# Convolution rows through DRAM, a list ordered behind a pair of state updates, and 2.2 instead of 1.83 gather slots to 16 tokens of a build

## The chip, the cores and the metric

The kernel runs on one core of a Trainium2 chip. Its time is the device time of one execution in microseconds (us), median of three runs; the profile is that of one more execution. The core has TensorE (PE in the profile; PEld are its weight loads), VectorE (DVE), ScalarE (ACT), GpSimd (POOL), SyncE (SP, which only issues DMA here) and 16 DMA engines.

## What is computed

One layer: RetNet retention and a Conformer convolution share an input projection and an output projection; a PEER layer follows, which picks 16 experts of 16,384 for each of 8 heads by product keys. The inputs are a prompt of 512 tokens and 8 sampled sequences of 4 new tokens, each with a retention state and 30 cached convolution rows. Cut to what matters here:

```python
def retention(q, k, v, r0, log_gamma):          # chunks of 128 tokens
    ...
    def step(r, kv_n):
        return chunk_decay * r + kv_n, r         # the state's update
    ...

def conformer_conv(ca, cg, buf, dw_kernel, dw_bias, ln_g, ln_b):
    u = ca * jax.nn.sigmoid(cg)
    xpad = jnp.concatenate([buf, u], axis=1)
    y = lax.conv_general_dilated(xpad, dw_kernel[:, None, :], window_strides=(1,), padding='VALID',
        dimension_numbers=('NWC', 'WIO', 'NWC'), feature_group_count=CONV_WIDTH) + dw_bias   # 31 taps, 512 channels
    return jax.nn.silu(layer_norm(y, ln_g, ln_b)), xpad[:, -(CONV_K - 1):]

def peer(x2d, w_query, sub_keys_1, sub_keys_2, peer_u, peer_v):
    ...
    v1, i1 = lax.top_k(s1, PEER_TOPK)
    v2, i2 = lax.top_k(s2, PEER_TOPK)
    cand = (v1[..., :, None] + v2[..., None, :])...
    sv, ci = lax.top_k(cand, PEER_TOPK)
    ...
    act = jax.nn.gelu(jnp.einsum('phkd,pd->phk', u, xb), approximate=False)
    return jnp.einsum('phk,phkd->pd', gate * act, vv)
```

## The kernel before

The prompt's first 128 tokens (the first chunk) go through everything up to their expert lists first; the 32 sampled tokens and the other 384 prompt tokens follow. Experts are applied in two ways. For 256 of the later tokens every expert is multiplied densely, in 128 blocks (scores `sp`, L1021; products `pB`, L1216), with gates from matrices that are *built* on TensorE from the lists: for each token `B` (two halves, L1138) and `A` (L1117 or on ScalarE, L1122) are made, and L1157 multiplies them. For all other tokens an expert is a *slot*: GpSimd issues an indirect DMA that fetches for each of 128 tokens one expert's row of 2 x 1024 numbers (L730), VectorE takes the dot product (L736), ScalarE the gelu and the gate (L748, L753), and VectorE accumulates (L758). The first chunk has 128 slots (indices `I`), the sampled tokens 32 (`Is`, on 128 partitions), the last 128 prompt tokens 128 (`Ib`).

The first chunk's lists are made by five calls of `retrieve`, on heads 0, 1, 2-3, 4-5 and 6-7. Each takes the best 16 keys of both sides, converts their indices (L658), forms candidate sums (L663), and picks the best 16 with one-hot comparisons (L682 to L689). The list is copied to `I` at L866.

The stage that the change is about runs from 160 to 240 us. Two generators are woven there by `woven`, which advances one and then the other:

- `later_conv`, for the 384 later prompt tokens: four channel blocks `m` of the gated product `u_p` (`glu`: two projections, L255; sigmoid on ScalarE, L285; product on VectorE, L290); then the convolution as matmuls (`conv_taps`, L336), and the value projections (`project_v`, L384) between them. Four taps at a time are contracted over 128 partitions, 4 x 32 channels, so a tile of *rows* is needed that holds the channels of one block four times, each copy shifted by one token: `tap_rows` makes it with 16 copies of 32 x 412 on ScalarE (L325) per block, and the tap weights with one product on VectorE (L327). Two places of the tile `blk` hold the rows of even and of odd blocks in turn.
- `retain_s`, the sampled tokens' retention: for each pair of sequences the query against the state (L506), the key-value product (L512) and the state's update on VectorE (L514). The updates are appended to the list `updates`, sixteen in all, two for each pair of heads. The states lie in the tiles `states`, `xr` (of the first chunk) and `keys`; a pair's states are loaded at L472 and written out at L518.

The program's order on each engine is made when it is built, by a scheduler that goes by data dependences, priorities and a model of times; each engine then works through its own order strictly. `behind(a, b)` orders `a` after `b`. Two tables order the slots. SLOTS_BEHIND holds pairs (k, i): every dot from the k-th of the first chunk's dots so far on stands behind the i-th update. TURNS = (24, 1.83) does it for the last 128 slots during the second build: slot k from 24 on stands behind the build's turn int((k - 24) // 1.83) + 1, where a turn is 16 tokens.

Transfers issued by SyncE go out in its order: weights of the input projection (L152), states and results among them.

## Time and profile before

| | before |
|---|---|
| time, median of 3 runs (lowest to highest) | 1458.32 us (1458.04 to 1463.03) |
| the profiled execution's own time | 1455.97 us |
| its span | 1454.2 us |
| mean granted TensorE clock | 0.987 |
| moved by DMA | 506.78 MB, 348 GB/s over the span |

The profile is read on three levels. The page gives the busy time of each engine as a share of the span, and the chain of work that ended last, followed back from the end. A busy share is an average over stages with different limits, so the stages are read apart: a window gives the busy time of every engine in a stretch, the granted clock and the DMA share. Within a stage the timeline shows each instruction (or a run of equal ones, xcount) with its start, its length, and, in brackets, the idle time of its engine ahead of it and what ended that. A group has busy time, mean ns of one, and the idle time ahead of its instructions. L numbers are lines of the kernel before; behind the change the same lines stand some 8 to 15 lines further down (L325 has gone, and the others become L327 → L336, L336 → L345, L384 → L393, L506 → L515, L512 → L521, L514 → L523, L518 → L527, L658 → L667, L736 → L745, L758 → L767, L1117 → L1132, L1138 → L1153, L1157 → L1172, L1216 → L1231).

### The profile page before, as it was taken

What the parts mean: (1) busy time and instruction counts of PE and PEld (TensorE: products, weight loads), DVE (VectorE), ACT (ScalarE), POOL (GpSimd) and SP (SyncE); (2) the same over time, 40 slices, a digit from 0 to 9 for tenths busy, and PEclk for the clock granted to TensorE, in tenths of its full rate; (3) what the DMA queues carried; (4) which work ended last, traced back from release to release, by engine and by line L of the source; (5) the groups of instructions that cost most, each with busy time, mean ns of one, the idle gap of its engine ahead of it and who ended that gap; (6) DMA issues with size and microseconds to landing.
All of it is one profiled execution on the core that took longest, in us unless ns stands there. A gap on an engine that the chain in (4) does not pass through costs nothing.

```text
span 1454.2 us, 19716 instructions
## 1 busy us (share of the span) xinstructions
PE 1404.1 (97%) x6758; PEld 963.9 (66%) x6758; DVE 1162.1 (80%) x2796; ACT 492.8 (34%) x1455; POOL 427.4 (29%) x407
## 2 busy tenths in 40 slices
PE   8999889999999999998999999999999989999997
PEld 8887455568767588887888884444445656566443
DVE  5849858987769999979999996987676887666656
ACT  1424773363122232244555541214444211111111
POOL 2172124233432333222133312333221333222220
PEclk9999989999999999999999999999999999999999
DMA  9859759987898799998799989999998999999995
GB/s 350 311 203 376 247 204 385 369 327 282 322 396 319 265 364 402 377 405 316 238 405 366 370 309 359 415 416 384 334 359 327 378 418 418 415 392 412 414 397 197
DMA packets 100401, 506.78 MB, mean 348 GB/s; under 512 B 10279, under 2 KB 21287, under 8 KB 57413
## 3 DMA queue, kind: packets, MB, share of 16 engines
q0 software_dynamic: 43392, 309.32, 54.4%
q1 hardware_dynamic: 52157, 190.10, 34.4%
q10 hardware_dynamic: 4752, 6.11, 1.2%
q8 instruction: 53, 0.87, 0.2%
q14 instruction: 47, 0.39, 0.1%
HBM read 500.12 MB, written 5.80 MB: 348 GB/s over the span
## 4 chain that ended last, share of the span: by engine, by line
PE 50%; DVE 24%; DMA 14%; issue 5%; ACT 4%; POOL 1%; DVEq 0%; ACTq 0%; SPq 0%; POOLq 0%
PE pB L1216 25%; PE sp L1021 12%; PE mm L255 6%; DVE acc L758 6%; DMA g<-in_uv_dram,Ib 4%; DVE g L736 4%; DMA g<-in_uv_dram,I 4%; DMA uv<-in_ut_dram 3%; DVE g L316 2%; ACT blk L325 2%; PE mm L1157 2%; PE mm L583 1%; PE mm L336 1%; DMA cst<-in_consts_dram 1%; DMA ln<-in_uv_dram,I 1%
## 5 line engine op out<-in xcount | busy, mean ns | idle before, releaser
L1021 PE MATMUL sp<-x1T,uv 128*128 128x256 f32 x2048 | 465.8, 384 | 13.2 <-ACT W L1170 6.1
L1021 PEld LDWEIGHTS sp<-x1T,uv 128*128 128x128 f32 x2048 | 386.0, 191 | 81.8 <-issue 15.1
L758 DVE SCALAR_TENSOR_TENSOR acc<-g,wgt,acc 128x1024 f32<-128x1024 f32 x252 | 322.4, 1279 | 66.5 <-ACT wgt L753 64.5
L736 DVE SCALAR_TENSOR_TENSOR g<-g,x 128x1024 f32<-128x1024 f32 x255 | 309.0, 1217 | 77.3 <-DMA g<-in_uv_dram,Ib 49.4
L730 POOL DMA_INDIRECT g<-in_uv_dram,Ib x126 | 150.6, 1195 | 394.2 <-DVE acc L758 116.8
L748 ACT ACTIVATE act<-act 128x1 f32<-128x1 f32 x288 | 57.0, 201 | 577.6 <-DVE g L736 539.9
L730 POOL DMA_INDIRECT g<-in_uv_dram,I x104 | 135.9, 1307 | 296.9 <-DVE acc L758 176.9
L1216 PE MATMUL pB<-uv,Ga 128*128 128x512 f32 x352 | 158.7, 597 | 0.0
L255 PE MATMUL mm<-x1T,w 128*128 128x384 f32 (+1 forms) x448 | 152.9, 498 | 0.0
L255 PEld LDWEIGHTS mm<-x1T,w 128*128 128x128 f32 x448 | 84.5, 190 | 63.0 <-issue 31.6
L1216 PEld LDWEIGHTS pB<-uv,Ga 128*128 128x128 f32 x352 | 65.5, 190 | 70.8 <-issue 66.5
L1216 PE MATMUL pB<-uv,Gb 128*128 128x512 f32 x256 | 110.5, 593 | 0.0
L1216 PE MATMUL pB<-uv,Gd 128*128 128x512 f32 x256 | 110.0, 592 | 0.0
L1216 PEld LDWEIGHTS pB<-uv,Gb 128*128 128x128 f32 x256 | 48.3, 190 | 61.5 <-issue 57.1
L1216 PEld LDWEIGHTS pB<-uv,Gd 128*128 128x128 f32 x256 | 48.6, 190 | 60.9 <-issue 59.6
L1122 ACT ACTIVATE A<-row,e1T 128x128 f16<-128x128 bf16 x216 | 66.0, 391 | 45.5 <-PE mm L1157 45.1
L1216 PE MATMUL pB<-uv,Gc 128*128 128x512 f32 x160 | 71.5, 599 | 0.1
L255 PE MATMUL mm<-g,w 128*128 128x160 f32 (+1 forms) x512 | 65.3, 287 | 0.0
L255 PEld LDWEIGHTS mm<-g,w 128*128 128x128 f32 x512 | 64.4, 191 | 0.6
L730 POOL DMA_INDIRECT g<-in_uv_dram,Is x25 | 31.6, 1266 | 75.3 <-DVE acc L758 43.4
L1216 PEld LDWEIGHTS pB<-uv,Gc 128*128 128x128 f32 x160 | 29.3, 190 | 34.8 <-issue 33.0
L1170 ACT ACTIVATE W<-sp 128x256 f32<-128x256 f32 (+25 forms) x84 | 26.4, 314 | 73.2 <-PE sp L1021 70.9
(328 smaller groups left out, 1732.7 us busy)
## 6 DMA issues: line engine op xcount, KB each, us to landing
uv<-in_ut_dram SPq DMA_DIRECT2D x128, 512.0 KB
uv<-in_uv_dram SPq DMA_DIRECT2D x128, 512.0 KB
w<-in_w_in_dram SPq DMA_DIRECT2D x18, 1024.0 KB
w<-in_w_query_dram SPq DMA_DIRECT2D x15, 1024.0 KB
w<-in_w_out_dram SPq DMA_DIRECT2D x7, 1024.0 KB
ln<-in_ln_g_dram POOLq DMA_DIRECT2D x5, 512.0 KB
ln<-in_ln_b_dram POOLq DMA_DIRECT2D x5, 512.0 KB
g<-in_uv_dram,Ib POOLq DMA_INDIRECT x126
```

What stands on the lines that cost most here:

```text
L255: T.matmul(p[:, :n], w[m // 2][:, k, (m % 2) * 128:(m % 2 + 1) * 128], xT[:, k, c0:c0 + n], start=(k == 0), stop=(k == 7))
L316: V.scalar_tensor_tensor(y[:, m], u_p[:, m, p0 + k:p0 + k + L], dw[:, m, k:k + 1], y[:, m], op0=OP.mult, op1=OP.add)
L325: S.activation(rows[j * 32:j * 32 + 32, g], u_p[g * 32:g * 32 + 32, m, p0 + j:p0 + j + w], AF.Copy)
L730: fetch = G.indirect_dma_start(out=t, out_offset=None, in_=a["uv"], in_offset=bass.IndirectOffsetOnAxis(ap=idx[:, k:k + 1], axis=0))
L736: dot = V.scalar_tensor_tensor(t[:, :D], t[:, :D], 1.0, x1, op0=OP.mult, op1=OP.mult, accum_out=act[:, 0:1])
L748: gate_ = S.activation(act[:, 1:2], act[:, 0:1], AF.Gelu)
L758: V.scalar_tensor_tensor(acc, v, wgt, acc, op0=OP.mult, op1=OP.add)
L1021: mm = T.matmul(sp[:, i], u[:, k], x1T[:, k, NG2:], start=(k == 0), stop=(k == 7), skip_group_check=True)
L1122: made = S.activation(A[:, t], row, AF.Abs, bias=e1T[:, t1 + t:t1 + t + 1])
L1157: mm = T.matmul(pt[:, t % nt], A[t % TB], B[:, q, t % TB // 2, :, t % 2], start=(q == 0), stop=(q == 1))
L1170: S.activation(W[:, :n], sp[:, :n], AF.Gelu)
L1216: return [T.matmul(pB[b][q], W[:, b * 128:(b + 1) * 128], vt[:, q * 512:(q + 1) * 512], start=False, stop=(e == NK - 1), skip_group_check= ...
```

## The change

Four things. The row tiles of the convolution are no longer copied by ScalarE: each finished channel block of `u_p` is stored to DRAM (`store_u`, one DMA of 128 x 415 on ScalarE's queue, L322), and read back by four DMAs on SyncE's queue (L330), one for each shift, 32 partitions x 4 x 412. The loads are placed earlier than the copies were: those of a block go ahead of the block before it in the second loop. The tap weights are a function of their own. The conversion L658 of each list is kept in `placed`, and that of the first chunk's last list is ordered behind the first pair of state updates. And the two tables change their numbers. By TURNS, TensorE's order in the second build has for the most part 8 value products (two matmuls each in the profile) between the matmuls of 16 tokens, or 4 between those of 8, where it had 10; in VectorE's order dots and accumulations now stand between the two halves of some tokens' `B` too.

```diff
@@ -40,8 +40,8 @@
 FREE = 8
 TB_AT = {30: (0, 1), 36: (1, 1), 42: (2, 2), 50: (4, 2), 88: (6, 2)}
 SECOND = 34
-SLOTS_BEHIND = ((7, 1), (8, 3), (11, 5), (12, 7), (14, 9))
-TURNS = (24, 1.83)
+SLOTS_BEHIND = ((7, 1), (8, 3), (10, 5), (11, 7), (13, 9))
+TURNS = (24, 2.2)
 TURN = (90, 92)
 S_AT = 8
 GATED = 116
@@ -123,7 +123,7 @@
     banks = [ps0]
     turn = [0]
 
-    steps, updates = {}, []
+    steps, u_dram, updates, placed = {}, {}, [], []
 
     def mmps():
         turn[0] += 1
@@ -316,17 +316,26 @@
                 V.scalar_tensor_tensor(y[:, m], u_p[:, m, p0 + k:p0 + k + L], dw[:, m, k:k + 1], y[:, m],
                                        op0=OP.mult, op1=OP.add)
 
-    def tap_rows(m, L, p0, place):
+    def store_u(m, L, p0):
+
+        u_dram[m] = dr.tile([128, L + CK], F32, name=f"u_dram{m}")
+        nc.scalar.dma_start(u_dram[m], u_p[:, m, p0:p0 + L + CK])
+
+    def tap_rows(m, L, place):
 
         w = L + CK - 3
         rows = place[:, 0:4 * w].rearrange("p (g t) -> p g t", g=4)
-        for g in range(4):
-            for j in range(4):
-                S.activation(rows[j * 32:j * 32 + 32, g], u_p[g * 32:g * 32 + 32, m, p0 + j:p0 + j + w], AF.Copy)
+        by_group = u_dram[m].rearrange("(g c) t -> c g t", g=4)
+        for j in range(4):
+            nc.sync.dma_start(rows[j * 32:j * 32 + 32], by_group[:, :, j:j + w])
+        return rows
+
+    def tap_weights(m):
+
         taps = small("taps", [128, 32, 32], bufs=1)
         V.tensor_tensor(taps, cc("eye32").unsqueeze(1).to_broadcast([128, 32, 32]),
                         dwt[:, m].rearrange("p g k -> p (g k)").unsqueeze(2).to_broadcast([128, 32, 32]), op=OP.mult)
-        return rows, taps.rearrange("p (g k) c -> p g k c", g=4)
+        return taps.rearrange("p (g k) c -> p g k c", g=4)
 
     def conv_taps(y, m, L, rows, taps):
 
@@ -655,7 +664,7 @@
                 first = top16(vv[:n, j, s], iu[:n, j, s], sb[:n, s], NK)
                 if later:
                     later(first)
-        V.tensor_tensor(fi[:n], iu[:n], unit_k[:n].unsqueeze(1).unsqueeze(3).to_broadcast([n, nh, 2, TK]), op=OP.mult)
+        placed.append(V.tensor_tensor(fi[:n], iu[:n], unit_k[:n].unsqueeze(1).unsqueeze(3).to_broadcast([n, nh, 2, TK]), op=OP.mult))
         cand = pick("cand", [128, 2, nh, NCAND], bufs=1)
         both, src = cand.rearrange("p q h c -> p (q h) c"), vf.rearrange("p q h s k -> p (q h) s k")
         off = 0
@@ -891,17 +900,22 @@
         rows = {}
         for m in range(4):
             glu(W0[5], wca, xT, L, p0, ms=[m])
+            store_u(m, L, p0)
             yield
+            if m in (1, 3):
+                rows[m // 2] = tap_rows(m // 2, L, room[m // 2])
             if m == 1:
-                rows[0] = tap_rows(0, L, p0, room[0])
+                taps = tap_weights(0)
             if m == 2:
-                yield from conv_taps(y, 0, L, *rows[0])
+                yield from conv_taps(y, 0, L, rows[0], taps)
         w = load_win(2)
         for m in range(1, 4):
-            rows[m] = tap_rows(m, L, p0, room[m % 2])
+            if m < 3:
+                rows[m + 1] = tap_rows(m + 1, L, room[(m + 1) % 2])
+            taps = tap_weights(m)
             vs.append(project_v(w, xT, 128 * (m - 1)))
             yield
-            yield from conv_taps(y, m, L, *rows[m])
+            yield from conv_taps(y, m, L, rows[m], taps)
 
     banks[:] = [ps]
     r = slice(NS, n)
@@ -910,6 +924,7 @@
     for k, i in SLOTS_BEHIND:
         for dot in dots[k:]:
             behind(dot, updates[i])
+    behind(placed[4], updates[1])
     banks[:] = [ps]
     rope(load_win(0), 0, xT, n - NS, 160, [(0, n - NS, qT)])
     later_keys = rope_steps(load_win(1), 1, xT, n - NS, 160, [(0, n - NS, kT)])
```

Where the instructions stand now. In VectorE's order around the last list (names: `states` are the first pair's states, L514 and L523 their updates; `vf` is written by the conversion that starts a list's second half, L658 and L667; `u_p` is a gated product). Before, from the conversion to the first updates, with the rows between left to the sentence behind:

```order
L758 SCALAR_TENSOR_TENSOR acc<-g,wgt,acc 128x1024
L658 TENSOR_TENSOR vf<-iu,unit_k 128x64
L687 TENSOR_TENSOR oh<-oh 128x32x24
L696 TENSOR_TENSOR GT_135<-ex,sm 128x32
L663 TENSOR_TENSOR cand<-vf 128x4x16
```

```order
L686 TENSOR_TENSOR oh<-oh,ci 128x1600
L696 TENSOR_TENSOR GT_135<-ex,sm 128x32
L514 SCALAR_TENSOR_TENSOR states<-states,mm 128x2x128 x2
L687 TENSOR_TENSOR oh<-oh 128x32x24
L736 SCALAR_TENSOR_TENSOR g,act<-g,x_0_132 128x1024
L688 TENSOR_TENSOR oh<-oh 128x32x12
L689 TENSOR_REDUCE E_134<-oh 128x32
```

Behind the change:

```order
L698 TENSOR_REDUCE E_134<-oh 128x32
L875 CAST I_136<-E_134 128x32
L290 SCALAR_TENSOR_TENSOR u_p<-mm,cols,sg 128x384
L523 SCALAR_TENSOR_TENSOR states<-states,mm 128x2x128 x2
L667 TENSOR_TENSOR vf<-iu,unit_k 128x64
L745 SCALAR_TENSOR_TENSOR g,act<-g,x_0_132 128x1024
L672 TENSOR_TENSOR cand<-vf 128x4x16
```

The first pair's updates stood 27 rows behind the conversion, near the end of the last list; now they stand right ahead of the conversion, and the list before is finished ahead of them.

In TensorE's order of the same stage (L506 and L515 read the states, L512 and L521 multiply keys and values, L336 and L345 are the convolution's matmuls, L384 and L393 the value projection, L255 a projection). Before:

```order
L255 MATMUL mm<-x1T,w 128x384 x8
L506 MATMUL mm<-states,on 32x128 x8
L336 MATMUL mm<-blk,taps 32x384 x8
L512 MATMUL mm<-on,ktok 128x256 x2
L336 MATMUL mm<-blk,taps 32x384 x16
L506 MATMUL mm<-xr_862,on 32x128
L512 MATMUL mm<-on,ktok 128x256 x2
L506 MATMUL mm<-xr_862,on 32x128 x7
L336 MATMUL mm<-blk,taps 32x384 x8
L255 MATMUL mm<-x1T,blk 128x384 x7
```

Behind the change:

```order
L255 MATMUL mm<-x1T,w 128x384 x8
L515 MATMUL mm<-states,on 32x128 x8
L521 MATMUL mm<-on,ktok 128x256 x2
L515 MATMUL mm<-xr_862,on 32x128 x8
L521 MATMUL mm<-on,ktok 128x256 x4
L345 MATMUL mm<-blk,taps 32x384 x32
L255 MATMUL mm<-x1T,blk 128x384 x8
L255 MATMUL mm<-x1T,w 128x384 x8
L521 MATMUL mm<-on,ktok 128x256 x2
L393 MATMUL mm<-w,x1T 128x256 x16
```

The convolution's matmuls of block 0 lay between the key-value products; now they follow three pairs of these in one piece.

SyncE's order in the stage (L152 loads weights, L472 and L481 load states, L518 and L527 write them out). Before:

```order
L152 DMA w<-in_w_in_dram 128x2048 x5
L472 DMA keys<-in_state_retention_dram 128x8x128 x2
L518 DMA out_dram<-states 128x8x128
L152 DMA w<-in_w_in_dram 128x2048
L518 DMA out_dram<-xr_862 128x8x128
L518 DMA out_dram<-keys 128x8x128 x2
```

Behind the change (u_dram_1807, 1838, 1871 and 1976 are the stored blocks 0 to 3):

```order
L152 DMA w<-in_w_in_dram 128x2048 x5
L330 DMA blk<-u_dram_1807 32x4x412 x4
L527 DMA out_dram<-states 128x8x128
L330 DMA blk<-u_dram_1871 32x4x412 x4
L330 DMA blk<-u_dram_1838 32x4x412 x4
L481 DMA keys<-in_state_retention_dram 128x8x128 x2
L152 DMA w<-in_w_in_dram 128x2048
L527 DMA out_dram<-xr_862 128x8x128
L330 DMA blk<-u_dram_1976 32x4x412 x3
L527 DMA out_dram<-keys 128x8x128
L330 DMA blk<-u_dram_1976 32x4x412
L527 DMA out_dram<-keys 128x8x128
```

The row loads of three blocks, and a write of states, now stand ahead of the load of the last states and of a weight tile.

## The prediction, made before the changed kernel was run

> **What bounds the kernel now.** I read the page first (span, busy shares, the chain that ended last), then the busy times by stage, then TensorE's timeline in the stage that the edited lines run in, and last the timelines of ScalarE and VectorE at TensorE's two waits there. The profiled execution took 1455.97 us, 1.77 more than its span and 2.35 less than the median of the runs, 1458.32.
>
> ```profile
> span 1454.2 us, 19716 instructions
> PE 1404.1 (97%) x6758; PEld 963.9 (66%) x6758; DVE 1162.1 (80%) x2796; ACT 492.8 (34%) x1455; POOL 427.4 (29%) x407
> PE 50%; DVE 24%; DMA 14%; issue 5%; ACT 4%; POOL 1%; DVEq 0%; ACTq 0%; SPq 0%; POOLq 0%
> ```
>
> TensorE is busy for 97% of the span, but VectorE and DMA together hold 38% of the chain: the limit changes from stage to stage. So each edit has to be priced in its own stage. The columns of the next rows are the stretch, its length, the busy time of TensorE, its weight loads, VectorE, ScalarE and GpSimd, the granted TensorE clock, the DMA share and GB/s. First comes the convolution of the later tokens, then the stage behind it, then a stage that VectorE fills.
>
> ```profile
> 159.60:240.50 80.90, 70.49 (x482) 40.09 (x481) 61.01 (x125) 46.19 (x103) 25.18 (x21) 0.89 0.72 251
> 240.50:345.00 104.50, 101.26 (x433) 70.26 (x430) 90.36 (x165) 48.51 (x114) 36.26 (x32) 0.98 0.87 339
> 440.00:640.00 200.00, 200.00 (x890) 160.74 (x889) 194.27 (x627) 59.62 (x172) 59.31 (x46) 1.00 0.92 351
> 170.00:180.00 10.00, 9.54 (x48) 5.12 (x48) 9.74 (x19) 6.01 (x15) 1.25 (x2) 0.74 0.80 228
> 200.00:210.00 10.00, 5.00 (x29) 2.49 (x28) 9.30 (x16) 1.49 (x6) 4.13 (x4) 0.62 0.78 286
> ```
>
> The first stage is slack on every side: TensorE idle for 10.4 us of 80.9, VectorE for 19.9, a DMA share of 0.72, and a clock of 0.89. The last two rows show where the clock goes: 0.74 and 0.62 right after TensorE's waits. TensorE's rows there, with those that give each kind of matmul at full rate:
>
> ```profile
> 159.57 0.64 PE L506 MATMUL mm<-states,on 128*32 128x128 f32 x16
> 161.43 0.70 PE L512 MATMUL mm<-on,ktok 32*128 32x256 f32 x4
> 170.46 1.55 PE L512 MATMUL mm<-on,ktok 32*128 32x256 f32 x4 [5.41 <-DVE states L514]
> 181.44 5.32 PE L255 MATMUL mm<-x1T,w 128*128 128x384 f32 x16
> 205.04 1.22 PE L512 MATMUL mm<-on,ktok 32*128 32x256 f32 x2 [5.00 <-DVE keys L514]
> 231.69 3.62 PE L384 MATMUL mm<-w,x1T 128*128 128x256 f32 x16
> 235.24 5.37 PE L336 MATMUL mm<-blk,taps 128*32 128x384 f32 x64
> 240.54 20.91 PE L255 MATMUL mm<-x1T,w 128*128 128x384 f32 x64
> ```
>
> At those rates the stage's matmuls (the busy groups below give the larger counts) need 256/64 x 5.37 = 21.5 us for L336, 96/16 x 3.62 = 21.7 for L384, 2 x 5.32 = 10.6 for L255, 4 x 0.64 = 2.6 for L506 and 8 x 0.70 = 5.6 for L512: 62.0 us. From 159.57 to 240.54 it took 81.0. So **19 us are lost**: 10.4 idle and 8.6 in matmuls at a lower clock.
>
> ```profile
> L336 PE MATMUL mm<-blk,taps 128*32 128x384 f32 x256 | 26.6, 532 | 0.0
> L384 PE MATMUL mm<-w,x1T 128*128 128x256 f32 x96 | 23.1, 394 | 0.0
> L512 PE MATMUL mm<-on,ktok 32*128 32x256 f32 x32 | 9.6, 497 | 10.4 <-DVE states L514 5.4 <-DVE keys L514 5.0
> ```
>
> Both waits are for a states' update (L514) of VectorE. Why those were late:
>
> ```profile
> 163.14 0.22 DVE L658 TENSOR_TENSOR vf<-iu,unit_k 128x64 f32<-128x64 uint32 x1
> 169.99 0.74 DVE L514 SCALAR_TENSOR_TENSOR states<-states,mm 128x256 f32<-128x256 f32 x2
> 191.62 0.62 DVE L290 SCALAR_TENSOR_TENSOR u_p<-mm,cols,sg 128x384 f32<-128x384 f32 x1 [10.07 <-ACT sg L285]
> 198.09 1.28 DVE L758 SCALAR_TENSOR_TENSOR acc<-g,wgt,acc 128x1024 f32<-128x1024 f32 x1 [5.20 <-ACT wgt L753]
> ...
> 176.90 12.79 ACT L325 ACTIVATE blk<-u_p 32x412 f32<-32x412 f32 x23
> 191.00 0.58 ACT L285 ACTIVATE sg<-mm,cols 128x384 f32<-128x384 f32 x1
> 191.61 3.76 ACT L325 ACTIVATE blk<-u_p 32x412 f32<-32x412 f32 x7
> ```
>
> The first pair stood in VectorE's order behind the first chunk's last list, which runs from 163.14 to 170, though its matmuls were done by 162.13. The second wait starts on ScalarE: 23 row copies hold the sigmoid of the last channel block until 191.00, VectorE idles 10.07 us for it, seven more copies hold the gathers' weights, VectorE idles 5.20 more, and then works off dots and accumulations ahead of the update that TensorE takes at 205.04.
>
> **The change part by part.** *The list behind the first pair.* The pair now follows the third gate product (L290) directly. What stays ahead of it from 153.0 on, summed from VectorE's timeline, is 9 us at most, so it runs near 162, where TensorE is ready at 160.5 to 161 (the matmuls of the convolution that lay between have moved behind): a wait of about 1.5 us instead of 5.41. The second pair stands behind one dot and the seven candidate sums, so some 2 us of wait there, and some 2 at a later pair that stands behind a dot: 5 us of short waits are left (an estimate; the ends are 0 and the 10.4 of before). The list itself, 7 us of work, comes later by the instructions that passed it, and costs nothing: its slots are the last 32 of the first chunk's 128, and the gathers before them cover it.
>
> *The copies.* 64 copies leave ScalarE:
>
> ```profile
> L325 ACT ACTIVATE blk<-u_p 32x412 f32<-32x412 f32 x64 | 34.7, 544 | 4.9 <-DVE u_p L290 2.4 <-PE mm L336 1.7
> ```
>
> With them goes what held the sigmoid and the weights, so both VectorE idles (15.3 us) and TensorE's second wait with its slow matmuls. In their place ScalarE issues four stores, each waiting for its gate product. Gelus and gather weights queue behind that wait; it is bounded by one dot and one accumulation ahead of the product (2.5 us), and ScalarE has 35 us more room. Cost taken: nothing, at most 2.5 us each.
>
> *The transfers.* Four stores of 128 x 415 x 4 bytes are 0.85 MB; sixteen loads write 128 x 412 x 4 bytes, 3.37 MB: together 4.22 MB. Their price at a full DMA, and on a queue whose packets are of their size:
>
> ```profile
> 230.00:240.00 10.00, 10.00 (x86) 6.26 (x88) 9.40 (x14) 1.50 (x6) 5.83 (x5) 1.00 1.03 414
> 160.00:170.00 10.00, 5.05 (x62) 1.88 (x54) 10.00 (x45) 5.94 (x8) 2.88 (x2) 0.92 0.65 211
> q10 hardware_dynamic: 4752, 6.11, 1.2%
> ```
>
> 414/1.03 = 402 GB/s make it 10.5 us; 211/0.65 = 325 GB/s make it 13.0. The third row has packets of 1.29 KB on average, against 1.65 KB for a row of 412 values: 6.11 MB in 1.2% of 1454.2 us, 350 GB/s, so 12.0 us, which I take. The stage held DMA for 0.72 x 80.9 = 58.2 us; with 12.0 more it is 70.2, so DMA alone allows a gain of 10.7, and a little more where a transfer slides into the next stage (share 0.87). By the worst bound, with two more gather slots (2.1 MB, 5 us) pulled in, it is 76, a gain of 5.
>
> The Trainium skill's page "DMA: Bandwidth & Descriptors", section "Measured (HBM→SBUF, 128 partitions, SWDGE, issued from GpSimd)", speaks against this: it asks for batches of 1 MiB or more for 75% of peak, and these loads are 211 KB. At half rate (an estimate) the 4.22 MB would take 21 us, the stage 79 to 84, and no gain would be left. The queue of 1.29 KB packets above, at 350 GB/s, does not bear that out here.
>
> Does a row tile come late? Its latency is bounded by a gather, from its issue to the dot that waited for it:
>
> ```profile
> 199.64 1.68 POOL L730 DMA_INDIRECT g<-in_uv_dram,I  x1 [11.40 <-DVE acc L758]
> 206.01 1.22 DVE L736 SCALAR_TENSOR_TENSOR g<-g,x 128x1024 f32<-128x1024 f32 x1 [0.70 <-DMA g<-in_uv_dram,I]
> ```
>
> 6.4 us. The rows of block 0 are loaded a whole gate product ahead, those of 2 and 3 one block (some 20 us) ahead. Only those of block 1 are tight: they wait for the last read of a weight tile, and have 5.3 (L255) + 0.7 + 7.2 (32 of L384) = 13 us of cover. SyncE's queue is in order, so the loads of the sampled states and of the next weights stand behind them and inherit that wait. Taken: nothing; 6.4 us if the cover fails.
>
> *Slots per turn, 1.83 to 2.2.* In the second build the matmuls of 16 tokens now stand 16 value matmuls apart instead of 20:
>
> ```profile
> 1052.85 0.56 PE L1157 MATMUL mm<-B,ss 128*128 128x32 f16 x16
> 996.58 7.11 PE L1216 MATMUL pB<-uv,Gc 128*128 128x512 f32 x16
> 1062.32 0.56 PE L1157 MATMUL mm<-B,A 128*128 128x32 f16 x16
> 1063.13 8.83 PE L1216 MATMUL pB<-uv,Ga 128*128 128x512 f32 x20
> 1053.79 0.69 DVE L1117 TENSOR_TENSOR ss<-iot,e1H 128x1024 f16<-128x1024 f16 x1 [2.37 <-PE mm L1157]
> 1058.56 2.69 DVE L758 SCALAR_TENSOR_TENSOR acc<-g,wgt,acc 128x1024 f32<-128x1024 f32 x2 [0.26 <-ACT wgt L753]
> 985.00:1125.00 140.00, 140.00 (x822) 71.32 (x821) 98.87 (x189) 65.25 (x201) 33.04 (x28) 1.00 0.93 349
> 1125.00:1270.00 145.00, 137.09 (x457) 86.47 (x457) 110.50 (x200) 27.02 (x97) 49.57 (x37) 0.98 1.00 407
> ```
>
> By that TensorE's period falls from 9.47 us to 9.47 - (8.83 - 7.11) = 7.75. VectorE needs 1053.79 to 1061.25, 7.5 us, for a unit with two slots, and 0.2 slots more (1.22 + 1.28 each) make 8.0. So TensorE will wait some 0.2 us a unit, over 16 units 4 us. In return the stage from 1125 on, where DMA is full and TensorE lost 7.9 us, has fewer slots left to fetch. The total of matmuls is unchanged, and by the last unit only one dot more has been done. I take 0, between -2.5 (one slot's VectorE time) and +4.
>
> **Sum.** PE alone allows 19 - 5 = 14 us, DMA 10.7, the rest nothing: **11 us**. What follows the stage shifts as a whole: VectorE, which sets the end of 440 to 640 (194 of 200 us busy), is freed of its 15.3 us of idle time too. 1455.97 - 11 = 1445.0, and 2.35 more for the median: 1447.
>
> **Rivals.** *DMA-bound.* The loads are dear and delay gathers; the stage ends at 76 to 81. For it: 1.65 KB pieces; against it: the 1.29 KB queue. Gain 0 to 5, 1453 to 1458.
> *Given back.* Stages behind are bound by DMA (shares 0.87 to 0.92) and VectorE; the earlier start only turns into waits for gathers, and the extra 12 us of transfers remain. Gain 0 to 3, about 1457. Against it: slots are dotted earlier as well.
> *The build waits.* Dots stand between the halves of B in VectorE's order, so a gather that is late holds B, and TensorE with it. Bytes for it: a slot is 1.05 MB; 349 GB/s over 9.47 us less two slots leave 1.2 MB of weights to 20 matmuls, 0.96 to 16; with 2.2 slots that is 3.27 MB in 7.75 us, 422 GB/s, over the 407 that the full stage moved. At 16 units, 0.7 us of wait each eats the 11 us; from (11 + 7.3)/16 = 1.15 us each it is slower: about 1468. Against it: the 0.3 us that DMA's rate alone adds.
> *Shorter waits that cost as the long ones.* The row of clock 0.62 follows 5.00 us of idle time. If three waits of 2 us each cost 8.6/2 = 4.3 us of slow matmuls, 13 us go, and the gain is 1: 1457. No row of the stage shows a slow clock after a wait that short. The Trainium skill ("TensorE: Matmul & The Clock Gate", section "Part 1: The HAM clock gate") has the clock drop after about one idle window of 3.4 us, which would leave short waits free; both long waits here exceed it, and agree.
>
> **How the numbers follow.** Forecast (gain 8 to 20): 0.62. DMA-bound: 0.12. Given back, or short waits dear: 0.14. The build waits: 0.12. Half a per cent, 7.3 us, is about what a measurement of this kernel can tell from no change. Faster by more: nearly all of the forecast and a little besides, 0.64; same: 0.25; slower: 0.11. The range: the best case is 19 + 2.5 = 21.5, so 1437; upward it takes in both rivals without a gain (1458) and a build that waits slightly: 1460.
>
> **What would show it.** L325 gone from ScalarE; TensorE's L512 (now L521) idle of 10.4 falling below 6; the clock from 0.89 to above 0.95 in the stage; the stage from 81 to about 70; DMA share there near 1.0. Wrong if the convolution's matmuls (L345) wait for the row tiles, if the first dense pass starts no earlier, or if the matmuls L1172 show a wait for B of over 0.7 us a unit.

## The result, and the profile after

The changed kernel took 1445.33 us (median of 5 runs, 1441.51 to 1450.86) against 1459.11 before (5 runs, 1458.04 to 1463.62): a ratio of 0.9897, with a 95% interval of 0.9864 to 0.9931. That is 13.8 us less by the medians. The profiled execution took 1442.01 us. Two of the experiments had a disturbed (slow) execution, the profiled one; it is left out of their times, and their kernels were run a second time for a profile.

The page of the changed kernel, its span, busy shares and chain by engine:

```profile
span 1440.2 us, 19685 instructions
PE 1398.3 (97%) x6758; PEld 963.1 (67%) x6758; DVE 1161.1 (81%) x2796; ACT 463.3 (32%) x1392; POOL 417.4 (29%) x407
PE 45%; DVE 28%; DMA 17%; issue 5%; POOL 2%; ACT 2%; SPq 0%; DVEq 0%; POOLq 0%
```

TensorE's busy time fell by only 5.8 us, ScalarE's by 29.5. Windows of the changed kernel come next (columns as above): the stage of the convolution, from the first matmul on the states to the first projection behind it; then the next stage; then the stretch from the 257th to the 705th matmul `pB`, which holds the second build and the stage behind it.

```profile
161.30:236.90 75.60, 66.48 (x483) 38.30 (x482) 60.12 (x121) 17.36 (x50) 23.85 (x21) 0.93 0.98 330
237.00:345.00 108.00, 108.00 (x472) 76.94 (x473) 98.35 (x177) 52.60 (x123) 38.91 (x35) 1.00 0.91 354
970.90:1260.10 289.20, 285.67 (x1314) 164.47 (x1313) 218.59 (x406) 97.61 (x304) 77.23 (x68) 1.00 0.99 391
```

The same last stretch of the kernel before:

```profile
977.20:1274.80 297.60, 289.63 (x1312) 164.64 (x1313) 218.96 (x405) 93.58 (x303) 87.38 (x68) 0.99 0.97 379
```

So the stage of the convolution takes 75.6 us instead of 81.0, not the 70 of the prediction; and the stretch around the second build, for which the prediction had put down nothing, takes 289.2 us instead of 297.6. **5.4 us came from the one place, 8.4 from the other.** (These are two single executions. The changed kernel comes to the stage 1.7 us later, and this start lies between 157.8 and 162.1 in all the profiles; its stretch between the two places is 2.6 us shorter, and the rest behind them 0.7 us longer. The experiments below measure the two parts over more executions.)

TensorE's timeline of the changed kernel shows why the stage kept so much of its loss:

```profile
164.47 1.03 PE L521 MATMUL mm<-on,ktok 32*128 32x256 f32 x4 [1.33 <-DVE states L523]
167.10 1.55 PE L521 MATMUL mm<-on,ktok 32*128 32x256 f32 x4 [1.61 <-DVE states L523]
173.08 6.76 PE L345 MATMUL mm<-blk,taps 128*32 128x384 f32 x64 [4.43 <-DMA blk<-u_dram]
```

The waits for the first updates are the 1.5 and 2 us that were forecast. But ahead of the convolution stands a new wait of 4.43 us, for the row tile of block 0. The groups of the stage (busy time, mean ns | idle time ahead) say the same: 5.1 us of new idle time at L345, and 3.9 left of the 10.4 at the key-value products, with 7.4 us busy instead of 9.6, at a clock of 0.93 instead of 0.89 over the stage.

```profile
L345 PE MATMUL mm<-blk,taps 128*32 128x384 f32 x256 | 26.2, 513 | 5.1 <-DMA blk<-u_dram 4.4 <-DVE taps L336 0.6
L521 PE MATMUL mm<-on,ktok 32*128 32x256 f32 x32 | 7.4, 461 | 3.9 <-DVE states L523 2.9 <-DVE keys L523 0.8
```

### The profile page after: what moved, and what is told of

It is laid out like the page before. It is cut to its first block, busy times and chain, and to the rows that moved or that the text cites. A ratio compares the mean times of both kernels' runs of the same rounds, so it can differ in the third digit from the quotient of the medians.

```text
span 1440.2 us, 19685 instructions
## 1 busy us (share of the span) xinstructions
PE 1398.3 (97%) x6758; PEld 963.1 (67%) x6758; DVE 1161.1 (81%) x2796; ACT 463.3 (32%) x1392; POOL 417.4 (29%) x407
## 2 busy tenths in 40 slices
DMA packets 103281, 511.01 MB, mean 355 GB/s; under 512 B 10599, under 2 KB 24167, under 8 KB 60293
## 4 chain that ended last, share of the span: by engine, by line
PE 45%; DVE 28%; DMA 17%; issue 5%; POOL 2%; ACT 2%; SPq 0%; DVEq 0%; POOLq 0%
PE pB L1231 18%; PE sp L1036 13%; PE mm L255 9%; DVE acc L767 7%; DMA g<-in_uv_dram,Ib 5%; DVE g L745 5%; DMA g<-in_uv_dram,I 5%; DVE g L316 2%; DMA blk<-u_dram 1%; POOL g L739 1%; DMA ln<-in_uv_dram,I 1%; DMA cst<-in_consts_dram 1%; PE mm L1172 1%; DMA g<-in_uv_dram,Is 1%; PE mm L592 1%
## 5 line engine op out<-in xcount | busy, mean ns | idle before, releaser
L739 POOL DMA_INDIRECT g<-in_uv_dram,Ib x126 | 144.3, 1145 | 391.1 <-PE pB L1231 134.7
L739 POOL DMA_INDIRECT g<-in_uv_dram,I x104 | 133.0, 1279 | 305.9 <-DVE acc L767 180.1
L255 PE MATMUL mm<-x1T,w 128*128 128x384 f32 (+1 forms) x448 | 152.7, 498 | 0.0
L255 PEld LDWEIGHTS mm<-x1T,w 128*128 128x128 f32 x448 | 84.5, 190 | 63.2 <-issue 31.2
L255 PE MATMUL mm<-g,w 128*128 128x160 f32 (+1 forms) x512 | 65.3, 287 | 0.0
L255 PEld LDWEIGHTS mm<-g,w 128*128 128x128 f32 x512 | 64.4, 191 | 0.6
L739 POOL DMA_INDIRECT g<-in_uv_dram,Is x25 | 34.5, 1379 | 79.4 <-DVE acc L767 39.1
L1188 DVE TENSOR_TENSOR Gd<-Gd,W 128x256 f32<-128x256 f32 x32 | 13.5, 423 | 48.0 <-ACT W L1185 48.0
```

What stands on the lines that cost most here:

```text
L255: T.matmul(p[:, :n], w[m // 2][:, k, (m % 2) * 128:(m % 2 + 1) * 128], xT[:, k, c0:c0 + n], start=(k == 0), stop=(k == 7))
L739: fetch = G.indirect_dma_start(out=t, out_offset=None, in_=a["uv"], in_offset=bass.IndirectOffsetOnAxis(ap=idx[:, k:k + 1], axis=0))
```

## The experiments

All are measured against the kernel before, whose medians in these sessions were 1459.0 to 1461.9 us. Differences in us are worked out from the ratio, where nothing else is said. Line numbers are each kernel's own: L1157 and L336 in the kernels built on the one before, L1172 and L345 in those built on the changed one, and in some of either kind one more.

**The table of slots alone, e1_turns_only.**

```diff
-TURNS = (24, 1.83)
+TURNS = (24, 2.2)
```

> The kernel before with one number changed: 2.2 slots to 16 tokens of the second build. Theory A (the slots give more than half of the gain: between the first and the last sixteenth of the value products the changed kernel took 8.5 us less, and its wait of 5.20 us for W at 1181 is gone): 6 to 10 us faster than before, about 1451; the two idle spells of TensorE over 0.9 us behind 1125 us gone, and 3 us of short waits for B in the build instead. Rival B (my prediction: the table is worth nothing, -2.5 to +4 us, and the late difference is by chance of one run): 1457 to 1463, within noise of before.

Measured: 1449.59 us, ratio 0.9936 (0.9914 to 0.9958), 9.3 us faster. So one number in a table gives about two thirds of the whole. Its window, and the two kinds of wait of TensorE that are left in it, one row of each:

```profile
980.70:1268.10 287.40, 285.72 (x1312) 164.54 (x1313) 215.18 (x403) 96.64 (x303) 75.45 (x67) 1.00 0.99 390
```

```profile
1043.79 0.64 PE L1157 MATMUL mm<-B,ss 128*128 128x32 f16 x16 [1.08 <-DVE B L1138]
1180.64 3.69 PE L1021 MATMUL sp<-x1T,uv 128*128 128x256 f32 x16 [0.16 <-DMA uv<-in_ut_dram]
```

Against 297.6 us before, TensorE idles for 1.7 us in the window instead of 8.0, and its matmuls take 285.7 us instead of 289.6: what went is idle time and the slow matmuls behind it. What stood there before is seen where the dense scores follow the build. First TensorE, then ScalarE, then VectorE of the kernel before:

```profile
1181.09 5.88 PE L1021 MATMUL sp<-x1T,uv 128*128 128x256 f32 x16 [5.20 <-ACT W L1170]
1193.69 1.88 PE L1216 MATMUL pB<-uv,Ga 128*128 128x512 f32 x4
```

```profile
1175.33 0.20 ACT L748 ACTIVATE act<-act 128x1 f32<-128x1 f32 x1 [3.24 <-DVE g L736]
1179.10 0.20 ACT L748 ACTIVATE act<-act 128x1 f32<-128x1 f32 x1 [3.24 <-DVE g L736]
1180.68 0.36 ACT L1170 ACTIVATE W<-sp 128x256 f32<-128x256 f32 x1
```

```profile
1174.06 1.23 DVE L736 SCALAR_TENSOR_TENSOR g<-g,x 128x1024 f32<-128x1024 f32 x1 [0.65 <-DMA g<-in_uv_dram,Ib]
1177.83 1.22 DVE L736 SCALAR_TENSOR_TENSOR g<-g,x 128x1024 f32<-128x1024 f32 x1 [0.66 <-DMA g<-in_uv_dram,Ib]
```

The conversion W, which empties the bank that TensorE's next scores need, stands on ScalarE behind the gelus of late slots; each gelu waits for its dot, each dot for its gather; three of the four behind the W before come 3.8 us apart, at the pace of the gathers, while the matmuls for W had been done since 1172. TensorE waits 5.20 us, and then 16 matmuls take 5.88 us instead of 3.6. With 2.2 slots to 16 tokens the build is over earlier, and this row of waits is not there. Counted from the start of the window, the build's last matmul comes after 147.1 us before the change and after 132.4 us behind it, with 212 and 213 dots begun. The dots behind the build show the gathers directly; they are as many, but before the change VectorE idled 18.6 us for their gathers (first row, 1124.5 to 1274.8 us), and here 0.5 (second row, 1111.3 to 1268.1):

```profile
L736 DVE SCALAR_TENSOR_TENSOR g<-g,x 128x1024 f32<-128x1024 f32 x38 | 46.3, 1221 | 18.6 <-DMA g<-in_uv_dram,Ib 18.6
L736 DVE SCALAR_TENSOR_TENSOR g<-g,x 128x1024 f32<-128x1024 f32 x38 | 46.3, 1218 | 0.5 <-DMA g<-in_uv_dram,Ib 0.5
```

**Without the table, e2_no_turns.** The changed kernel with the old number.

```diff
-TURNS = (24, 2.2)
+TURNS = (24, 1.83)
```

> The changed kernel with 1.83 slots to 16 tokens again; all else as changed. Theory A: 4 to 7 us faster than before (1452 to 1455), what the stage of the convolution gave in the trace (1.72 us late at its start, 3.64 early at its end). Rival B: 10 to 14 us faster, as the whole change.

Measured: 1454.28 us, ratio 0.9963 (0.9943 to 0.9983), 5.4 us faster than before, as theory A has it. The wait is back in its place:

```profile
973.10:1270.20 297.10, 289.59 (x1313) 164.19 (x1314) 218.84 (x405) 93.56 (x303) 88.28 (x68) 0.99 0.97 379
```

```profile
1157.68 3.72 PE L1036 MATMUL sp<-x1T,uv 128*128 128x256 f32 x16 [0.95 <-ACT W L1185]
1176.66 5.32 PE L1036 MATMUL sp<-x1T,uv 128*128 128x256 f32 x16 [4.94 <-ACT W L1185]
```

**More slots, e8_turns_26, and fewer, e10_turns_15.** The kernel before, with this number alone changed.

```diff
-TURNS = (24, 1.83)
+TURNS = (24, 2.6)
```

> The kernel before with 2.6 slots to 16 tokens of the second build (2.2 in the change). If the gain is slots done before the stage in which DMA is full, it saturates: the wait for W is gone already at 2.2, and TensorE now waits for B more often (8.6 us of VectorE's work to a unit): 5 to 9 us faster than before, so up to 4 us slower than 2.2. Rival: more slots, more gain: 12 to 15 us faster.

```diff
-TURNS = (24, 1.83)
+TURNS = (24, 1.5)
```

> The kernel before with 1.5 slots to 16 tokens of the second build instead of 1.83, the other direction. If slots that are not done in the build are what holds W, and so TensorE, in the stage behind it (6 us of waits and some 2.5 us of slow matmuls at 1.83), fewer slots done there make it worse: more waits for W between 1150 and 1280 us, 3 to 12 us slower than before. Rival (the gain of 2.2 comes from the denser order of the build itself, not from the slots): the waits for W stay as they are and the time is within 3 us of before.

Measured: with 2.6 slots 1450.97 us, ratio 0.9928 (0.9906 to 0.9951), the same as with 2.2; with 1.5 slots 1469.70 us, ratio 1.0059 (1.0039 to 1.0080), 8.6 us slower. The windows over the same matmuls, 2.6 slots first:

```profile
983.10:1271.10 288.00, 286.19 (x1312) 164.06 (x1313) 215.21 (x403) 96.77 (x303) 75.33 (x68) 1.00 0.99 390
```

```profile
980.90:1284.00 303.10, 292.52 (x1312) 166.04 (x1313) 218.03 (x404) 95.55 (x304) 96.11 (x68) 0.98 0.95 368
```

With 1.5 slots TensorE waits for W three times over 1.8 us:

```profile
1228.00 5.41 PE L1021 MATMUL sp<-x1T,uv 128*128 128x256 f32 x16 [2.91 <-ACT W L1170]
1245.60 3.72 PE L1021 MATMUL sp<-x1T,uv 128*128 128x256 f32 x16 [1.87 <-ACT W L1170]
1263.99 6.41 PE L1021 MATMUL sp<-x1T,uv 128*128 128x256 f32 x16 [4.36 <-ACT W L1170]
```

So the stretch takes 303, 298, 287 and 288 us at 1.5, 1.83, 2.2 and 2.6 slots. The dots that have begun when TensorE starts a given product `pB`, counted in the four traces, go the same way:

```
slots to 16 tokens     1.5  1.83   2.2   2.6
513th product          202   206   211   211
577th product          214   217   223   223
641st product          229   235   236   236
```

From 1.5 to 1.83 the build ends at the same product (the 546th and the 548th) and only the dots differ, so it is the slots and not a denser build that shorten the waits there. From 1.83 to 2.2 both change: the build then ends at the 520th product. At 2.6 the traces show nearly the order of 2.2, so this run does not test whether still more slots would gain more. The slight loss by waits for B that was expected did not come (1.3 us of such waits, as at 2.2).

**The list's order, e3_order_only.** The copies stay on ScalarE. `placed` is the list of the lists' conversions.

```diff
-SLOTS_BEHIND = ((7, 1), (8, 3), (11, 5), (12, 7), (14, 9))
+SLOTS_BEHIND = ((7, 1), (8, 3), (10, 5), (11, 7), (13, 9))
...
+        placed.append(V.tensor_tensor(fi[:n], iu[:n], ...))
...
+    behind(placed[4], updates[1])
```

> The kernel before, with its copies on ScalarE, and only the last list's conversion ordered behind the first pair of updates, with the new numbers of the slots behind updates. Theory A (two independent waits, one for the list and one for the copies): TensorE's wait of 5.41 falls to 1 to 2 us and its slow matmuls behind it go, the wait of 5.00 at the third pair stays; 3 to 6 us faster than before. Rival C (the copies set the pace of the stage whatever the order is): the wait moves behind the copies, gain under 2 us.

Measured: 1453.25 us, ratio 0.9956 (0.9938 to 0.9974), 6.4 us faster: no less than all of the change but the table (5.4 us, e2). The edit holds the new numbers of SLOTS_BEHIND too; the two were not taken apart. TensorE's waits of over 1 us in the stage:

```profile
165.62 1.03 PE L512 MATMUL mm<-on,ktok 32*128 32x256 f32 x4 [1.02 <-DVE states L514]
192.19 1.48 PE L336 MATMUL mm<-blk,taps 128*32 128x384 f32 x10 [1.40 <-ACT blk L325]
202.24 1.55 PE L512 MATMUL mm<-on,ktok 32*128 32x256 f32 x4 [4.79 <-DVE keys L514]
```

The wait behind the list is gone, the one behind the copies stays, as theory A had it; the stage, from the first matmul on the states to the last of the convolution, takes 75.6 us, against 75.7 in the changed kernel. It does so with a DMA share of 0.74 where the changed kernel has 0.98:

```profile
159.30:234.90 75.60, 67.86 (x483) 38.36 (x482) 60.03 (x122) 45.76 (x101) 24.06 (x21) 0.95 0.74 256
```

**The rows through DRAM alone, e5_rows_only.** The changed kernel with the old numbers in both tables and without the list's order.

```diff
-SLOTS_BEHIND = ((7, 1), (8, 3), (10, 5), (11, 7), (13, 9))
-TURNS = (24, 2.2)
+SLOTS_BEHIND = ((7, 1), (8, 3), (11, 5), (12, 7), (14, 9))
+TURNS = (24, 1.83)
...
-    behind(placed[4], updates[1])
```

> The kernel before with the row tiles through DRAM alone: the old numbers in both tables, and the last list not ordered behind the updates. Theory F (the rows through DRAM are worth nothing by themselves; the order of the list gave the 5 us of the stage, since the wait for the copies is only exchanged for a wait for the rows): within 3 us of before, 1456 to 1462, with a wait of TensorE for the row tile or for the states of 4 to 8 us in the stage. Rival G (my prediction's second half: the copies cost the second wait and its slow matmuls, half of 19 us): 5 to 8 us faster than before.

Measured: 1455.07 us, ratio 0.9986 (0.9965 to 1.0007): no gain that can be told from none, as theory F has it by the ratio; the interval still allows a gain of 5 us, and the median is 1 us below F's band. The two longest waits of the stage:

```profile
164.36 1.55 PE L521 MATMUL mm<-on,ktok 32*128 32x256 f32 x4 [4.75 <-DVE states L523]
198.31 4.48 PE L345 MATMUL mm<-blk,taps 128*32 128x384 f32 x32 [3.08 <-DMA blk<-u_dram]
```

The wait for the list stays, and a wait for a row tile stands where the wait behind the copies was. (Its single profile has a stage of 77.4 us, so 3.7 us of the stage did go; the runs do not show them as a sure gain.) DMA's share in this stage is 1.02, so the prediction's rival "DMA-bound" (a stage of 76 us or more, a gain of 0 to 5) describes this run as well as theory F does; the runs do not part the two. That the rows bring nothing on top of the list's order is seen in two more pairs: the gain is 5.4 us with them (e2) and 6.4 without (e3), and the next run does the same for the whole change.

**The change without the rows, e9_no_rows.** The edit is e3's and e1's together.

```diff
-TURNS = (24, 1.83)
+TURNS = (24, 2.2)
...
+    behind(placed[4], updates[1])
```

> The changed kernel without its first part: the copies stay on ScalarE; the list is ordered behind the first pair of updates, and both tables have the new numbers. Theory F: the two gains that were measured apart (6.4 and 9.3 us) add up, 14 to 16 us faster than before, 1443 to 1446, as fast as the whole change. Rival G: 5 to 8 us slower than the whole change, about 1452.

Measured: 1441.63 us, ratio 0.9888 (0.9866 to 0.9910), 16.3 us faster. The second run of this kernel:

> The kernel of e9_no_rows once more, for its profile, which was disturbed. Theory F: 1440 to 1446; in the stage a wait for the updates of the third pair of 4 to 5 us, as in e3_order_only, and a stage of 74 to 76 us, as the changed kernel's 75.2; no wait over 1 us for W behind the build, as in e1_turns_only.

Measured again: 1444.87 us (two runs), ratio 0.9886. The two gains add up, and without its first part the change is as fast as with it (0.9897, 0.9864 to 0.9931). Its profile keeps the wait behind the copies and has no wait for W:

```profile
204.93 1.55 PE L512 MATMUL mm<-on,ktok 32*128 32x256 f32 x4 [4.79 <-DVE keys L514]
```

```profile
PE mm L1158 <- DVE B L1139: 5.6, 5, 3.9
PE mm L512 <- DVE keys L514: 4.8, 1, 4.8
PE sp L1022 <- ACT Gb L1173: 3.8, 4, 1.6
```

(The last fence has the first three rows of TensorE's list of waits over the whole span: us in total, times, longest. The waits for B in it are for the most part those of the first build; 1.3 us are left in the second.)

**Pieces of another size, e7_half_pieces and e4_wide_rows.** Why is the row tile late? Its loads go out from 151.2 us, 22 us before the matmuls get it; the first piece starts at 154.8, the last is in at 172.4. The rows of the trace's DMA table, counted in stretches of 3 us: pieces of the row loads (1648 bytes, 512 to a block), and pieces of the gathers (8192 bytes).

```
start us   152  155  158  161  164  167  170  |  185  188
row loads   10  105  109   97  104   70   17  |  284  402
gathers     31   69   99   97  112  103   32  |   36    0
```

Beside gathers the row loads get on by some 100 pieces in 3 us, about one for each piece of a gather; without them (loads of the same size for blocks 2 and 1, from 185) by 280 to 400. So beside gathers it may be pieces that count, and not bytes. The Trainium skill (page "DMA: Bandwidth & Descriptors", section "Queues, rings and completion order") has a DMA engine take turns between the queues that have work, a packet of some 9 to 17 descriptors at a time. The like counts of the two kinds agree with turns (97 and 97 from 161 to 164); counts over 3 us do not show how many pieces make a turn.

To test it, half pieces, twice as many:

```diff
-            nc.sync.dma_start(rows[j * 32:j * 32 + 32], by_group[:, :, j:j + w])
+            for t in (0, w // 2):
+                nc.sync.dma_start(rows[j * 32:j * 32 + 32, :, t:t + w // 2], by_group[:, :, j + t:j + t + w // 2])
```

> The changed kernel with each row load cut in two halves of 206 tokens: the same bytes in twice as many pieces, 1024 of 824 bytes for a block. Theory D (a turn per piece beside the gathers): the first block's rows take some 18 us longer, TensorE's wait before the convolution rises from 4.43 to 15 to 22 us, and the kernel is 8 to 15 us slower than the changed one (1453 to 1460). Rival E (bytes or the queue decide): the wait stays at 3 to 6 us.

And pieces four times as large, by a layout in DRAM in which a partition's four rows follow one another:

```diff
-        u_dram[m] = dr.tile([128, L + CK], F32, name=f"u_dram{m}")
-        nc.scalar.dma_start(u_dram[m], u_p[:, m, p0:p0 + L + CK])
+        u_dram[m] = dr.tile([32, 4, L + CK], F32, name=f"u_dram{m}")
+        for g in range(4):
+            nc.scalar.dma_start(u_dram[m][:, g], u_p[g * 32:g * 32 + 32, m, p0:p0 + L + CK])
...
-        w = L + CK - 3
+        w = L + CK
...
-        by_group = u_dram[m].rearrange("(g c) t -> c g t", g=4)
+        by_group = u_dram[m].rearrange("c g t -> c (g t)")
...
-            nc.sync.dma_start(rows[j * 32:j * 32 + 32], by_group[:, :, j:j + w])
+            nc.sync.dma_start(place[j * 32:j * 32 + 32, 0:4 * w - 3], by_group[:, j:j + 4 * w - 3])
```

> The changed kernel with the stored block laid out so that a partition's four rows lie behind one another in DRAM: each row load is 128 pieces of 6.6 KB instead of 512 of 1.65 KB, the store 4 DMAs instead of one, bytes the same. Theory D (a row load takes one turn per piece beside the gathers' 8 KB pieces: in the changed kernel 100 pieces of 1648 bytes in every 3 us from 155 to 170, 300 to 400 where no gather ran): the first block's rows land 10 us earlier, TensorE's wait of 4.43 us before the convolution falls below 1 us, and the stage ends 3 to 5 us earlier. Rival E (the rows are late because their load stands behind five weight loads of 1 MB on SyncE's queue): the wait stays at 3 to 5 us, no gain.

```
start us        152  155  158  161  164  167  170
half pieces     137  133  115  109   12  362  156
 gathers         67  115  114  122   89    5   99
pieces of 6.6K    0   30   42   38   18    0    0
 gathers         12  116   54   61   86  142   42
```

Half pieces: 109 to 137 pieces in 3 us up to 164, as many as before or a few more, so some 0.6 of the bytes, as D has it. This run has two flaws as a test. SyncE issued four of block 0's eight loads by 152 and the other four only from 165.2 on, behind the write of the first states, and those got through by 171 because the gathers paused from 167 on (362 pieces). And TensorE's order came out otherwise: more key-value products, with waits of 2.95 and 1.90 us, stand ahead of the convolution. So the wait forecast for block 0 did not come; another block had one of 6.76 us:

```profile
211.70 6.88 PE L346 MATMUL mm<-blk,taps 128*32 128x384 f32 x64 [6.76 <-DMA blk<-u_dram]
```

The stage took 88.5 us, 12.8 more than in the changed kernel, but the kernel 1444.10 us, ratio 0.9910 (0.9878 to 0.9941): it was not 8 to 15 us slower, and theory D's forecast failed there. In its profile 6.6 of the 12.8 us had been made up by the 257th product `pB` (the stretches up to the first dense scores and from there on are 3.2 and 3.4 us shorter). Time in the stage is only partly time of the kernel.

Pieces of 6.6 KB: the load is through by 167 us, though it went out later (at 153.8 instead of 151.2), and no wait for the rows of block 0 is left. From its first piece's start to its last one's end it took 9.2 us in 128 pieces, against 17.6 in 512. At this size the pieces did not keep step with the gathers (30 to 42 beside 54 to 116), so the count alone does not set the pace either. And the stage still takes 75.5 us, at a DMA share of 0.99; a wait has moved:

```profile
160.80:236.20 75.40, 68.24 (x482) 37.97 (x481) 59.94 (x120) 18.30 (x52) 22.87 (x21) 0.93 0.99 328
198.46 0.64 PE L516 MATMUL mm<-keys,on 128*32 128x128 f32 x16 [3.37 <-DMA keys<-in_state_retention_dram]
```

The load of the last states stands behind the row loads of blocks 1 and 2 on SyncE's queue. Measured: 1442.91 us, ratio 0.9895 (0.9863 to 0.9928). The wait went as theory D has it; the gain of 3 to 5 us did not come. Whether the order of the loads or the full DMA holds the stage at 75 us is not shown.

**The waits mended together, e6_best.** As e4, with one store a block, the loads of block 2 behind those of the last states, and the load of the sampled tokens' x behind the last update.

```diff
+    for load in row_loads[2]:
+        behind(load, state_loads[-1])
...
-    nc.scalar.dma_start(xrs[0][:NS], a["x"][128:128 + NS])
+    behind(nc.scalar.dma_start(xrs[0][:NS], a["x"][128:128 + NS]), updates[-1])
```

> The changed kernel with rows of 6.6 KB pieces, one store for each block, the loads of block 2 ordered behind the loads of the last states, and the load of the sampled tokens' x (which held ScalarE for 12.99 us) ordered behind the last update. If what is left of the stage's loss is these waits: TensorE idle for under 4 us in the stage, which takes 68 to 71 us instead of 75, and 3 to 6 us faster than the changed kernel (1439 to 1442). Rival: DMA bound (a share of 0.98 in the stage already), 75 us as before and no gain over the changed kernel.

Measured: 1455.69 us, ratio 0.9974 (0.9954 to 0.9995), so slower than the changed kernel. The second run of this kernel:

> The kernel of e6_best once more, whose profiled execution was disturbed (a clock of 0.675) so that its waits can't be read. If its 12 us against e4_wide_rows are real, the time is 1452 to 1460 again and the trace shows a stretch behind the stage in which TensorE idles or runs at a lower clock for 8 to 14 us more than in e4_wide_rows, most likely where the sampled tokens' x is awaited (330 to 400 us); if they were the chip's, it is 1440 to 1446.

Measured again: 1452.34 us, ratio 0.9948 (0.9923 to 0.9974). Not a better version. TensorE waits for ScalarE in the stage, and ScalarE did not get to the store of the last block before 197.17:

```profile
200.54 1.08 PE L516 MATMUL mm<-keys,on 128*32 128x128 f32 x16 [5.93 <-ACT wgt L763]
```

```profile
197.17 0.53 ACTq L322 DMA_DIRECT2D u_dram<-u_p  x1
197.74 0.40 ACT L509 ACTIVATE on<-v,cst 128x128 f32<-128x128 f32 x1 [15.40 <-DMA blk<-u_dram]
```

The stage took 78.9 us, and the 200 us behind it up to the first dense scores 5 us more than in e4 (197.9 against 192.8). Which of the three edits did that was not taken apart.

No version beat the changed kernel by more than the intervals: e4, e9 and the change itself lie at 0.9886 to 0.9897.

## Why the prediction came out as it did

The time (1447 forecast, 1445.33 measured), the sign and the range held. The sum behind it did not: it put all of its 11 us into the stage and nothing into the second build, and the profiles show 5.4 and 8.4. So two of its terms were far off, and that their errors nearly cancelled was luck. One of the prediction's own signs of being wrong came: the convolution's matmuls waited for a row tile.

- *The first wait, behind the list*: right in mechanism and size. The pair's update came at 164.0, not 162 (first row below); the waits of 1.5 and 2 us were 1.33 and 1.61. By e3, this part with its numbers in SLOTS_BEHIND is worth 6.4 us of time.
- *The copies, and with them the second wait*: the step that failed is "Does a row tile come late? ... Taken: nothing". The rows of block 0, "loaded a whole gate product ahead", arrived 22 us after the loads went out, with 18 us of pieces trickling beside the gathers. The 6.4 us of a gather were the wrong row to bound them by: a gather is 128 rows of 8 KB, a row load of a block 512 pieces of 1.65 KB, and in pieces a quarter as many it was through in half the time (e4). So the wait of 5.00 us was exchanged for one of 4.43, and e2, e5 and e9 agree that this part brings nothing that can be told from none.
- *The transfers*: the bytes were right (511.01 MB moved instead of 506.78), their price of 12.0 us too low. DMA's share times the stage's length rose from 58.2 us to 74.1 (0.98 of 75.6), 15.9 more. By that DMA alone would have allowed 7 us instead of 10.7 (an estimate from the two windows, which also hold transfers that moved in from other stages). The queue of 1.29 KB packets was priced over its own busy time, not beside gathers.
- *The store's wait on ScalarE*, bounded at 2.5 us: too small. ScalarE was idle for 4.46 us ahead of the instruction behind the second store (put down to the gate product) and for 6.61 at the fourth (put down to the landing of row loads, which the prediction did not reckon with):

```profile
164.01 0.74 DVE L523 SCALAR_TENSOR_TENSOR states<-states,mm 128x256 f32<-128x256 f32 x2
157.20 1.28 ACT L757 ACT_TABLE_LOAD   x1 [4.46 <-DVE u_p L290]
192.43 0.40 ACT L508 ACTIVATE on<-v,cst 128x128 f32<-128x128 f32 x1 [6.61 <-DMA blk<-u_dram]
```

- *The clock*: 0.93 in the stage, not above 0.95; the waits of 4.43 and 1.61 us are each followed by slow matmuls (the row at 167.10: 1.55 us for what takes 0.70; the row at 173.08: 6.76 for what takes 5.37). The rival that short waits cost slow matmuls too was partly right: the row is behind a wait of 1.61 us, but one of 1.33 had come 2.6 us ahead of it.
- *Slots per turn*, taken as 0: the term that failed, by 8 to 9 us. That TensorE would wait a little for B in the build was right (3.2 us in all). That "by the last unit only one dot more has been done" was right too (213 against 212), and the wrong measure: the unit itself came 15 us earlier in the stretch, and at the same product 5 or 6 dots more had begun. The prediction had the gain's place in its own rows, the stage from 1125 on where TensorE lost 7.9 us, and let it cancel against B. It did not follow the two idle rows there, ScalarE's W behind late gelus, to what made them late.
- *The rivals*: "the build waits" was wrong in sign. "DMA-bound" (a stage of 76 to 81 us, 1453 to 1458) is nearly what the change does without its table: 1454.28 us in e2, with a stage of 75.3. So the part that the forecast had priced at 11 us gave 5.4. That DMA is what holds the stage there is not shown: with the copies kept and DMA far from full, the stage is as long (e3).

## What to carry to other kernels

A table's one number can outweigh the edits around it: follow the idle rows of the stage that it feeds, back through the engine's order to the transfer that is late, and try the number in both directions, with a look in the trace at whether it still changes the order (2.6 hardly did). A copy between partitions that is replaced by a way through DRAM needs a price for its pieces beside the other traffic, by a queue of such pieces that ran beside the same traffic, not by its bytes alone. And a wait that is removed should be measured alone: here the list's order, with its numbers in SLOTS_BEHIND, gave the stage's whole gain.

## What had not been expected of the hardware

A load of 512 pieces of 1648 bytes took some 18 us beside gathers of 8 KB pieces, at about 100 pieces in 3 us, and halving the pieces left that count about where it was (109 to 137), while 128 pieces of 6.6 KB took 9 us. Loads of 1648-byte pieces run at 284 to 402 in 3 us with few gathers or none. And of 12.8 us by which one version's stage was longer, the kernel's ratio shows 2 us (0.9910 against 0.9897, with intervals of 0.3% on either side).
